# Start of a two-block transformer kernel: x loaded behind the second layer's first memory weights, squares of x on GpSimd, one key/value copy on VectorE

## The chip, the core and the metric

The kernel runs on one core of one Trainium2 chip. The metric is device time in microseconds (us) of one execution. Five engines each run their own instruction stream in order and meet only at semaphores: TensorE (PE, and PEld for its weight loads), VectorE (DVE), ScalarE (ACT), GpSimd (POOL) and SyncE (SP), which issues the DMAs here.

## The reference, cut to what matters

Two blocks of two layers each. The change touches only the first 80 us, where this is computed for the first block:

```python
for l in range(DEPTH):                       # DEPTH = 2, x is 512 x 1024, mem is 256 x 1024
    h = rms_norm(x, pre_norm[l])
    proj = h @ w_in[l]                       # all projections of the tokens
    ...
    mkv = rms_norm(mem, mem_norm[l]) @ w_mem_kv[l]   # keys and values of the memory
    mk, mv = jnp.split(mkv, 2, axis=-1)
```

`mkv` depends on no token, so the kernel computes it for both layers before anything else. `rms_norm` needs the sum of squares of each token, and that of `x` at the start is the one that the change moves to another engine.

## The kernel before

All matrices are kept transposed, with 1024 features as 8 chunks of 128 partitions. Products are made in split precision: each factor is a high part and a low part (the remainder), and a product is three matmuls (`mm3`, L353 to L355: high by high, low by high, high by low). For weights, ScalarE casts the high part (`wh`, L419) out of the loaded tile `wr`, and VectorE or GpSimd subtracts it to get the low part (`wl`, L421). For activations ScalarE writes `mh`, `xh` and VectorE `ml`, `xl`.

The program starts with these steps, in the order in which the code is written:

- `memory` (L903 on): for both layers l, two units u of 256 output columns, each from two halves of four chunks. A unit is 48 matmuls. Each half is one weight load of 512 KB (`wr`, one of two buffers). The row sums of squares of `mem` go through `square` (ScalarE squares, GpSimd adds), `ss_matmul` (L473, four matmuls against ones into `tp`) and `rsqrt` (nine tiny VectorE instructions, L364 to L372) to the factor `mr`. `finish` (L947 on) then copies the finished products out of PSUM with that factor (`mkv`, L952).
- `load_x`: four DMAs of 512 KB for x, called before the change in layer 0, behind the issue of the second unit's second weight half.
- `lead_load`: the weights of the first gate products, four loads (two halves of two units, called lead weights below: `wr_497`, `wr_507` for the first half of the features, `wr_517`, `wr_527` for the second). VectorE makes their low parts.
- `prenorm`: 16 chunks (8 feature chunks for each half of the tokens) through `pre_chunk`: ScalarE writes `xh`, VectorE `xl`, and `square` adds x squared to `sacc`.
- `lead` (192 matmuls into `sc`), then the token projections (`tok`, matmuls into `mm`), whose weight low parts (`wl_888` and on) GpSimd makes.

The written order isn't the final one: a scheduler of the framework reorders instructions on each engine by its own cost model when the program is built, so a change of engine or of call order can move others. Within an engine the final order is fixed, and an engine waits at the first instruction whose inputs aren't there. The weight tiles `wr` have two buffers, so a load of a token weight waits until GpSimd has split the one before the last; and all loads are issued from SP's single stream.

Of the kernel before, what the change touches and what calls it, by code (L numbers as in the profile page):

```python
# [23 lines left out]
F32 = mybir.dt.float32  # L24
F32R = mybir.dt.float32r
I32 = mybir.dt.int32
AF = mybir.ActivationFunctionType
OP = mybir.AluOpType
# [284 lines left out]
class Kern:  # L313
# [160 lines left out]
                                      start=i + tb == 0, stop=i == len(qs) - 1, skip_group_check=True)  # L474
        return p[:, 0, :2]

    def square(self, st, c, src, last=False):

        nc = self.nc
        if c == 0:  # L480
            st["acc"] = self.sq.tile([128, 256], F32, name="sacc", tag="sacc", bufs=4)
            nc.scalar.activation(st["acc"], src, AF.Square)
            return
        q = self.sq.tile([128, 512], F32, name="sq", tag="sq")[:, 0:256]
        nc.scalar.activation(q, src, AF.Square)
        if c < KC - 1 or not last:
            nc.gpsimd.tensor_tensor(st["acc"], st["acc"], q, op=OP.add)
        else:
            st["last"] = q
# [26 lines left out]
    def pre_chunk(self, st, c, g, sl):  # L516

        nc = self.nc
        hi, lo = [x[:, c, sl] for x in self.h]
        x = self.XT[:, c, sl]  # L520
        nc.scalar.activation(hi, x, AF.Copy, scale=self.gcol(g, c))
        nc.vector.scalar_tensor_tensor(lo, x, self.gcol(g, c), hi.bitcast(F32), op0=OP.mult, op1=OP.subtract)
        self.square(st, c, x)

    def rows(self, r, out=None):

# [376 lines left out]
    def memory(self):  # L903

        nc, ap = self.nc, self.ap
        self.mkv = []
        with self.tc.tile_pool(name="mem", bufs=1) as mp, self.tc.tile_pool(name="mem2", bufs=2) as mp2:
            mT = mp.tile([128, KC, N_MEM], F32, name="mT")
            load = lambda c: nc.sync.dma_start(mT[:, c:c + 2], ap["memT"][:, c:c + 2])
            load(0)  # L910
            r, late = None, []
            for l in range(self.nl1):
                kv = self.mempool.tile([128, MB, 512], F32, name=f"mkv{l}")
                self.mkv.append(kv)
                mh = mp2.tile([128, KC, N_MEM], F32R, name="mh", tag="mh")
                ml = mp2.tile([128, KC, N_MEM], F32R, name="ml", tag="ml")
                ps = []
                for u in range(2):
                    ps.append([(self.sc if (l + u) % 2 else self.mm)()[:, 0:256] for _ in range(MB)])
                    for half in range(2):  # L920
                        w = self.wload(ap["w_mem"][l, u, half], lo=nc.vector, raws=self.lead_pool if u else None,
                                       cut=l == 0 and u == 0)
                        if l == 0 and u == 0 and half == 0:
                            for c in (2, 4, 6):
                                load(c)
                        if l == 0 and u == 1 and half == 1:
                            self.load_x()
                        for i in range(4):
                            c = half * 4 + i
                            if u == 0:  # L930
                                g = self.gcol(G_MEM + l, c)
                                nc.scalar.activation(mh[:, c], mT[:, c], AF.Copy, scale=g)
                                nc.vector.scalar_tensor_tensor(ml[:, c], mT[:, c], g, mh[:, c].bitcast(F32),
                                                               op0=OP.mult, op1=OP.subtract)
                            for t in range(MB):
                                sl = slice(t * 128, (t + 1) * 128)
                                self.mm3(ps[u][t], (mh[:, c, sl], ml[:, c, sl]), w[i], c == 0, c == KC - 1)
                    if l == 0 and u == 0:
                        st = {}
                        for c in range(KC):  # L940
                            self.square(st, c, mT[:, c], last=True)
                    if late:
                        late.pop()()
                if l == 0:
                    r = self.sm(2, "mr")

                def finish(l=l, ps=ps, kv=kv):  # L947
                    if l == 0:
                        self.rms(st, r)
                    for u in range(2):  # L950
                        for t in range(MB):
                            nc.scalar.activation(kv[:, t, u * 256:(u + 1) * 256], ps[u][t], AF.Copy, scale=r[:, t:t + 1])  # L952
                late.append(finish)
            late.pop()()

# [657 lines left out]
```

## Time and profile before

| what | us |
|---|---|
| median of 3 runs | 2846.74 |
| range of the runs | 2845.9 to 2852.84 |
| the profiled execution's own time | 2845.98 |
| its span | 2844.0 |
| PE busy over the span | 2741.8 (96%) |

A timeline row reads: start, duration, engine, line, operation, output tile and input tiles, number of instructions merged, and in brackets how long the engine was idle before it and on whom it waited. A row for a stretch gives each engine's busy time in it, the clock that TensorE was granted (1.00 is 2.4 GHz, 0.50 is 1.2 GHz), the share of DMA capacity in use and GB/s. The profiled execution lies 0.8 us under the median, and 2.0 us of it lie outside the span.

### The profile page before, as it was taken

How to read it: one execution, taken by the hardware profiler on the slowest of the kernel's cores; microseconds unless marked ns; L12 is line 12 of the kernel's file. 1: busy time of each engine (PE TensorE's matmuls, PEld its weight loads, DVE VectorE, ACT ScalarE, POOL GpSimd, SP SyncE). 2: the span in 40 equal slices, each digit the busy share in tenths (PEclk: the TensorE clock that was granted, in tenths of full speed). 3: DMA queues.
4: the chain of work that ended last, by engine and by line, in shares of the span. 5: the costliest groups of instructions: out<-in, count | busy, mean ns of one | idle time of the engine just before them, and what ended most of it. 6: DMA issues, size and time to landing. Idle time of an engine off the chain costs nothing.

```text
span 2844.0 us, 42873 instructions
## 1 busy us (share of the span) xinstructions
PE 2741.8 (96%) x16080; PEld 2398.0 (84%) x16080; DVE 1412.6 (50%) x2988; ACT 1374.1 (48%) x2881; POOL 1356.5 (48%) x1327
## 2 busy tenths in 40 slices
PE   8999999999999999899999999999998899999998
PEld 8997899788888887898988888888887798888887
DVE  6589757986302266747630225312336747731132
ACT  5678547874333335657433334333334758433332
POOL 4553365424444455443544445444455543544545
PEclk9999999999999999999999999999999999999999
DMA  5111221112333222121223232233222120223332
GB/s 176 60 46 38 75 72 46 45 66 75 96 92 103 85 81 83 51 79 62 78 96 96 97 93 93 89 89 104 95 77 86 62 81 31 90 82 91 105 99 77
DMA packets 69280, 230.53 MB, mean 81 GB/s; under 512 B 8968, under 2 KB 11912, under 8 KB 68816
## 3 DMA queue, kind: packets, MB, share of 16 engines
q1 hardware_dynamic: 69072, 227.78, 24.5%
q8 instruction: 127, 2.08, 0.3%
q14 instruction: 81, 0.66, 0.1%
HBM read 225.51 MB, written 2.24 MB: 80 GB/s over the span
## 4 chain that ended last, share of the span: by engine, by line
PE 74%; DVE 15%; ACT 4%; issue 3%; POOL 2%; DMA 2%; SPq 0%; POOLq 0%; DVEq 0%; ACTq 0%
PE sc L354 11%; PE sc L353 11%; PE sc L355 11%; PE mm L355 11%; PE mm L353 11%; PE mm L354 11%; DVE xl L299 2%; PE sc L116 2%; PE tp L145 1%; DVE pl L149 1%; DVE XT L287 1%; DVE nm L192 1%; DVE E L204 1%; PE tp L817 1%; POOL wl L421 1%
## 5 line engine op out<-in xcount | busy, mean ns | idle before, releaser
L421 POOL TENSOR_TENSOR wl<-wr,wh 128x512 fp32r<-128x512 f32 x732 | 942.0, 1297 | 883.0 <-ACT wh L419 858.9
L419 ACT CAST wh<-wr 128x512 fp32r<-128x512 f32 x836 | 500.5, 612 | 722.8 <-PE sc L354 450.9
L354 PE MATMUL sc<-xl,wh 128*128 128x512 f32 (+1 forms) x1824 | 658.0, 361 | 16.3 <-DVE xl L299 16.2
L355 PE MATMUL sc<-xh,wl 128*128 128x512 f32 (+1 forms) x1824 | 654.5, 359 | 0.2 <-DVE wl L421 0.2
L353 PE MATMUL sc<-xh,wh 128*128 128x512 f32 (+1 forms) x1824 | 653.2, 360 | 0.0
L607 DVE TENSOR_TENSOR fg<-sc,R 128x512 f32<-128x512 f32 (+1 forms) x92 | 59.3, 644 | 747.6 <-PE sc L355 724.5
L354 PEld LDWEIGHTS sc<-xl,wh 128*128 128x128 f32 x1824 | 344.0, 189 | 72.1 <-DVE xl L299 20.7
L355 PEld LDWEIGHTS sc<-xh,wl 128*128 128x128 f32 x1824 | 344.2, 189 | 51.8 <-DVE wl L421 0.4
L353 PEld LDWEIGHTS sc<-xh,wh 128*128 128x128 f32 x1824 | 342.5, 189 | 51.5
L355 PE MATMUL mm<-ah,wl 128*128 128x512 f32 (+1 forms) x792 | 291.0, 367 | 6.5 <-POOL wl L421 6.5
L353 PE MATMUL mm<-ah,wh 128*128 128x512 f32 (+1 forms) x792 | 290.3, 367 | 1.9 <-ACT wh L419 1.9
L354 PE MATMUL mm<-al,wh 128*128 128x512 f32 (+1 forms) x792 | 289.3, 365 | 0.0
L353 PE MATMUL mm<-wh,xh 128*128 128x256 f32 x960 | 275.0, 286 | 0.0
L354 PE MATMUL mm<-wl,xh 128*128 128x256 f32 x960 | 273.2, 285 | 0.0
L355 PE MATMUL mm<-wh,xl 128*128 128x256 f32 x960 | 273.0, 284 | 0.0
L353 PE MATMUL mm<-xh,wh 128*128 128x512 f32 (+1 forms) x560 | 196.7, 353 | 10.5 <-DVE big L789 3.4
L355 PE MATMUL mm<-xh,wl 128*128 128x512 f32 (+1 forms) x560 | 194.8, 348 | 7.8 <-POOL wl L421 7.8
L354 PE MATMUL mm<-xl,wh 128*128 128x512 f32 (+1 forms) x560 | 193.9, 346 | 0.0
L354 PEld LDWEIGHTS mm<-wl,xh 128*128 128x128 f32 x960 | 184.1, 192 | 1.3
L353 PEld LDWEIGHTS mm<-wh,xh 128*128 128x128 f32 x960 | 183.9, 192 | 1.0
L355 PEld LDWEIGHTS mm<-wh,xl 128*128 128x128 f32 x960 | 184.0, 192 | 0.9
L355 PEld LDWEIGHTS mm<-ah,wl 128*128 128x128 f32 x792 | 149.2, 188 | 33.8 <-POOL wl L421 9.6
(348 smaller groups left out, 4878.1 us busy)
## 6 DMA issues: line engine op xcount, KB each, us to landing
wr<-in_ffn_in_dram SPq DMA_DIRECT2D x176, 512.0 KB, 3.3
wr<-in_ffn_out_dram SPq DMA_DIRECT2D x64, 512.0 KB, 3.6
wr<-in_mix_in_dram SPq DMA_DIRECT2D x56, 512.0 KB, 3.3
wr<-in_w_in_dram SPq DMA_DIRECT2D x48, 512.0 KB, 3.3
wr<-in_ffn_out_dram SPq DMA_DIRECT2D x32, 384.0 KB, 3.1
wr<-in_w_out_dram SPq DMA_DIRECT2D x16, 512.0 KB, 3.3
wr<-in_mix_out_dram SPq DMA_DIRECT2D x16, 512.0 KB, 3.3
Mb<-Md SPq DMA_DIRECT2D x16, 256.0 KB, 3.1
```

The lines of the kernel that those rows point to most:

```text
L116: nc.tensor.matmul(sc[:, e], q, kk[:, :n], start=j == 0, stop=j == len(self.K) - 1)
L145: nc.tensor.transpose(p[:, j * per + e], E[i + e][:, j * 128:(j + 1) * 128], self.k.ident)
L149: nc.vector.tensor_tensor(pl[:, :nk, sl], pv, ph[:, :nk, sl].bitcast(F32), op=OP.subtract)
L192: nc.vector.tensor_reduce(nm, sc, axis=AX.X, op=OP.max, negate=True)
L204: nc.vector.scalar_tensor_tensor(E[tb, 0], E[tb, 1], cc[:, i:i + 1], E[tb, 0], op0=OP.mult, op1=OP.add)
L299: self.put(self.nc.vector.scalar_tensor_tensor(lo, k.XT[:, j, sl], k.gcol(self.nxt[0], j), hi.bitcast(F32), op0=OP.mult, op1=OP.subtract))
L353: mm(out, lhs[0], rhs[0], start=start, stop=False, skip_group_check=shared)
L354: mm(out, lhs[0], rhs[1], start=False, stop=False, skip_group_check=shared)
L355: mm(out, lhs[1], rhs[0], start=False, stop=stop, skip_group_check=shared)
L419: nc.scalar.copy(hi[:, :m], raw[:, c:c + m])
L421: ins = eng.tensor_tensor(low[:, :m], raw[:, c:c + m], hi[:, :m].bitcast(F32), op=OP.subtract)
L607: nc.vector.tensor_tensor(g, ps[0], R[:, sl], op=OP.mult)
```

## The change

Three edits. `load_x` is called in the second layer's first unit, behind the issue of its second weight half, so that both halves of that unit are ahead of x on SP. `pre_chunk` squares x on GpSimd: one multiplication for each of the 16 chunks, and one addition for 14 of them, where ScalarE squared and GpSimd added. `finish` copies the second layer's four products out of PSUM on VectorE instead of ScalarE.

```diff
+    def square(self, st, c, src, last=False, pool=False):
         nc = self.nc
+        if pool:
+            if c == 0:
+                st["acc"] = self.sq.tile([128, 256], F32, name="sacc", tag="sacc", bufs=4)
+                nc.gpsimd.tensor_tensor(st["acc"], src, src, op=OP.mult)
+                return
+            q = self.sq.tile([128, 512], F32, name="sq", tag="sq")[:, 0:256]
+            nc.gpsimd.tensor_tensor(q, src, src, op=OP.mult)
+            nc.gpsimd.tensor_tensor(st["acc"], st["acc"], q, op=OP.add)
+            return
...
-        self.square(st, c, x)
+        self.square(st, c, x, pool=True)
...
-                        if l == 0 and u == 1 and half == 1:
+                        if (l, u, half) == (self.nl1 - 1, 0, 1):
                             self.load_x()
...
-                            nc.scalar.activation(kv[:, t, u * 256:(u + 1) * 256], ps[u][t], AF.Copy, scale=r[:, t:t + 1])
+                            o = kv[:, t, u * 256:(u + 1) * 256]
+                            if l:
+                                nc.vector.tensor_scalar(o, ps[u][t], r[:, t:t + 1], None, op0=OP.mult)
+                            else:
+                                nc.scalar.activation(o, ps[u][t], AF.Copy, scale=r[:, t:t + 1])
```

What the scheduler makes of it, at three places. Numbers in names tell buffers apart; brackets name whose semaphores an instruction waits for.

**Place 1, x.** SP at the loads of x. `wr_317` and `wr_359` are the second layer's first unit before, `wr_313` and `wr_355` the same two after. Before:

```order
L395 DMA wr_273<-in_w_mem_dram 128x1024 [waits DMAHW2_49]
L464 DMA XT_86<-in_xT_dram 128x1024 [waits DMAHW3_49]
L464 DMA XT_86<-in_xT_dram 128x1024 [waits DMAHW4_49]
L464 DMA XT_86<-in_xT_dram 128x1024 [waits DMAHW5_49]
L464 DMA XT_86<-in_xT_dram 128x1024 [waits DMAHW6_49]
L395 DMA wr_317<-in_w_mem_dram 128x1024 [waits DMAHW7_49,DVE_49]
L395 DMA wr_359<-in_w_mem_dram 128x1024 [waits DMAHW0_49,DVE_49]
```

SP at the same place after:

```order
L395 DMA wr_273<-in_w_mem_dram 128x1024 [waits DMAHW2_49]
L395 DMA wr_313<-in_w_mem_dram 128x1024 [waits DMAHW3_49,DVE_49]
L395 DMA wr_355<-in_w_mem_dram 128x1024 [waits DMAHW4_49,DMAHW7_49,DMAHW0_49,DVE_49]
L464 DMA XT_86<-in_xT_dram 128x1024 [waits DMAHW5_49]
L464 DMA XT_86<-in_xT_dram 128x1024 [waits DMAHW6_49]
L464 DMA XT_86<-in_xT_dram 128x1024 x2
L395 DMA wr_423<-in_w_mem_dram 128x1024 [waits DMAHW1_49,DVE_49]
```

The four loads of x now stand behind a weight load that waits for VectorE to free its buffer.

**Place 2, POOL and SP behind the squares.** `wl_888`, `wl_892`, `wl_898`, `wl_902` belong to the first token unit (`wr_885`, `wr_895`), `wl_1061` and `wl_1065` to the next (`wr_1058`). POOL before:

```order
L487 TENSOR_TENSOR sacc_580<-sacc_580,sq_609 128x256 [waits Activation_49,Pool_49]
L487 TENSOR_TENSOR sacc_580<-sacc_580,sq_614 128x256 [waits Activation_49,Pool_49]
L421 TENSOR_TENSOR wl_888<-wr_885,wh_887 128x512 [waits DMAHW3_49,PE_49,Activation_49]
L421 TENSOR_TENSOR wl_892<-wr_885,wh_891 128x512 [waits PE_49,Activation_49]
L421 TENSOR_TENSOR wl_898<-wr_895,wh_897 128x512 [waits DMAHW4_49,PE_49,Activation_49]
```

POOL after; 24 more multiplications and additions of the same two kinds stand ahead of these rows, 30 in all since the first load of x:

```order
L487 TENSOR_TENSOR sacc_580<-sacc_580,sq_599 128x256 [waits Pool_49]
L486 TENSOR_TENSOR sq_609<-XT_86 128x256
L487 TENSOR_TENSOR sacc_580<-sacc_580,sq_604 128x256 [waits Pool_49]
L486 TENSOR_TENSOR sq_614<-XT_86 128x256
L487 TENSOR_TENSOR sacc_580<-sacc_580,sq_609 128x256 [waits Pool_49]
L487 TENSOR_TENSOR sacc_580<-sacc_580,sq_614 128x256 [waits Pool_49]
L421 TENSOR_TENSOR wl_888<-wr_885,wh_887 128x512 [waits DMAHW3_49,Activation_49]
L421 TENSOR_TENSOR wl_892<-wr_885,wh_891 128x512 [waits Activation_49]
L421 TENSOR_TENSOR wl_898<-wr_895,wh_897 128x512 [waits DMAHW4_49,DVE_49,Activation_49]
L421 TENSOR_TENSOR wl_902<-wr_895,wh_901 128x512 [waits DVE_49,Activation_49]
L421 TENSOR_TENSOR wl_1061<-wr_1058,wh_1060 128x512 [waits DMAHW7_49,DVE_49,Activation_49]
L421 TENSOR_TENSOR wl_1065<-wr_1058,wh_1064 128x512 [waits DVE_49,Activation_49]
```

SP at the lead weights before:

```order
L395 DMA wr_507<-in_w_in_dram 128x1024 [waits DMAHW6_49,DMAHW2_49,DVE_49]
L395 DMA wr_517<-in_w_in_dram 128x1024 [waits DMAHW5_49,DVE_49]
L395 DMA wr_527<-in_w_in_dram 128x1024 [waits DMAHW6_49,DVE_49]
L395 DMA wr_1058<-in_w_in_dram 128x1024 [waits DMAHW3_49,Pool_49]
L395 DMA wr_1068<-in_w_in_dram 128x1024 [waits DMAHW4_49,Pool_49]
L395 DMA wr_1192<-in_w_in_dram 128x1024 [waits DMAHW1_49,Pool_49]
```

SP at the lead weights after:

```order
L395 DMA wr_507<-in_w_in_dram 128x1024 [waits DMAHW6_49,DMAHW2_49,DVE_49]
L395 DMA wr_1058<-in_w_in_dram 128x1024 [waits DMAHW7_49,DMAHW3_49,Pool_49]
L395 DMA wr_1068<-in_w_in_dram 128x1024 [waits DMAHW4_49,DMAHW0_49,Pool_49]
L395 DMA wr_1192<-in_w_in_dram 128x1024 [waits DMAHW7_49,Pool_49]
L395 DMA wr_517<-in_w_in_dram 128x1024 [waits DMAHW5_49,DVE_49]
L395 DMA wr_527<-in_w_in_dram 128x1024 [waits DMAHW6_49,DVE_49]
```

The second half of the lead weights has moved behind three loads that wait for POOL, `wr_1192` for `wl_1065`.

**Place 3, DVE ahead of the second layer's second unit.** `wl_426` to `wl_464` are that unit's four low parts, the small rows between them the memory's `rsqrt`. Before:

```order
L372 SCALAR_TENSOR_TENSOR mr_311<-rnt_407,mr_311 128x2 [waits DVE_49]
L421 TENSOR_TENSOR wl_320<-wr_317,wh_319 128x512 [waits DMAHW7_49,Activation_49]
L421 TENSOR_TENSOR wl_324<-wr_317,wh_323 128x512 [waits Activation_49]
L421 TENSOR_TENSOR wl_362<-wr_359,wh_361 128x512 [waits DMAHW0_49,Activation_49]
L421 TENSOR_TENSOR wl_366<-wr_359,wh_365 128x512 [waits Activation_49]
L421 TENSOR_TENSOR wl_426<-wr_423,wh_425 128x512 [waits DMAHW1_49,Activation_49]
```

DVE after, where eleven `xl` stand ahead of `wl_426` (these rows begin at the eighth of them, and the other four splits of the layer stand earlier):

```order
L531 SCALAR_TENSOR_TENSOR xl_85<-XT_86,gains_87,xh_84 128x256 [waits DMAHW0_49,Activation_49]
L531 SCALAR_TENSOR_TENSOR xl_85<-XT_86,gains_87,xh_84 128x256 [waits Activation_49]
L531 SCALAR_TENSOR_TENSOR xl_85<-XT_86,gains_87,xh_84 128x256
L531 SCALAR_TENSOR_TENSOR xl_85<-XT_86,gains_87,xh_84 128x256 [waits Activation_49]
L364 TENSOR_SCALAR rnx_406<-tp_401 128x2 [waits PE_49]
L421 TENSOR_TENSOR wl_426<-wr_423,wh_425 128x512 [waits DMAHW1_49,Activation_49]
L365 TENSOR_SCALAR mr_307<-rnx_406 128x2 [waits DVE_49]
```

The splits of the first unit moved ahead of x's work, those of the second unit behind most of it, and `mr` behind both. On PE the lead's rows are reordered too, so that only 53 of its 192 matmuls stand ahead of the first one that reads the second half of the lead weights (`wh_519`), with two token matmuls (on `wh_887` and `wl_888`) among them, and the other 139 behind it; from its 442nd instruction on PE's order is that of before.

## Rows read from the trace of the kernel before

**Rows 1.** The page's busy time of each engine, share of the span, instructions.

```profile
PE 2741.8 (96%) x16080; PEld 2398.0 (84%) x16080; DVE 1412.6 (50%) x2988; ACT 1374.1 (48%) x2881; POOL 1356.5 (48%) x1327
```

**Rows 2.** Stretches: PE, PEld, DVE, ACT, POOL busy; PEclk; DMA share; GB/s.

```profile
16.70:22.40 5.70, 5.70 (x50) 5.67 (x49) 5.70 (x14) 5.70 (x16) 0.65 (x1) 1.00 0.97 385
22.90:28.00 5.10, 0.50 (x2) 0.30 (x2) 4.90 (x15) 3.30 (x8) 2.40 (x4) 0.82 0.02 6
28.00:32.90 4.90, 4.88 (x23) 4.88 (x24) 3.67 (x6) 3.40 (x8) 0.00 (x0) 0.50 0.66 182
32.90:41.50 8.60, 8.60 (x73) 8.60 (x73) 5.91 (x9) 7.52 (x19) 3.41 (x4) 1.00 0.46 151
41.50:65.90 24.40, 24.18 (x201) 23.84 (x200) 10.30 (x21) 9.91 (x23) 13.94 (x16) 1.00 0.36 119
65.90:90.00 24.10, 24.10 (x204) 24.10 (x203) 10.11 (x37) 10.01 (x17) 15.17 (x29) 1.00 0.13 45
```

**Rows 3.** The chain that ended last, in order of time: start, duration, what.

```profile
27.27 0.70 DVE wl L421
28.02 0.58 PE sc L354
```

**Rows 4.** PE's timeline at the lead's last matmuls and the first token matmul.

```profile
65.65 0.28 PE L354 MATMUL sc<-xl,wh 128*128 128x256 f32 x1
65.77 0.28 PE L355 MATMUL sc<-xh,wl 128*128 128x256 f32 x1
65.89 0.28 PE L353 MATMUL mm<-wh,xh 128*128 128x256 f32 x1
```

**Rows 5.** SP's timeline: the first load of x and the fourth memory unit's load.

```profile
6.60 0.33 SPq L464 DMA_DIRECT2D XT<-in_xT_dram  x1
13.13 0.33 SPq L395 DMA_DIRECT2D wr<-in_w_mem_dram  x1
```

**Rows 6.** Loads in 0 to 100 us, median to landing; then all `wr` loads, extremes.

```profile
wr<-in_w_in_dram SPq DMA_DIRECT2D x13, 512.0 KB, 3.4
DMA to landing us min/median/max: 3.3/5.2/8.3
```

**Rows 7.** POOL's instructions by line: duration ns min/median/max, starts, shape.

```profile
L487 POOL TENSOR_TENSOR sacc<-sacc,sq x116: 727/742/1302, 7.8 to 2827.8; 128x256 f32<-128x256 f32 x116
L1112 POOL TENSOR_TENSOR dsq<-pa x6: 1042/1042/1044, 161.3 to 569.6; 128x512 f32<-128x512 f32 x6
L421 POOL TENSOR_TENSOR wl<-wr,wh x6: 1289/1295/1307, 51.2 to 59.1; 128x512 fp32r<-128x512 f32 x6
```

**Rows 8.** POOL's timeline while DVE works too.

```profile
41.51 1.28 POOL L487 TENSOR_TENSOR sacc<-sacc,sq 128x256 f32<-128x256 f32 x1 [0.80 <-ACT sq L485]
42.94 0.74 POOL L487 TENSOR_TENSOR sacc<-sacc,sq 128x256 f32<-128x256 f32 x1
43.76 0.80 POOL L487 TENSOR_TENSOR sacc<-sacc,sq 128x256 f32<-128x256 f32 x1
```

**Rows 9.** DVE's timeline in the same stretch.

```profile
42.11 0.96 DVE L522 SCALAR_TENSOR_TENSOR xl<-XT,gains,xh 128x256 fp32r<-128x256 f32 x1
43.23 0.73 DVE L522 SCALAR_TENSOR_TENSOR xl<-XT,gains,xh 128x256 fp32r<-128x256 f32 x1 [0.16 <-ACT xh L521]
44.05 1.07 DVE L421 TENSOR_TENSOR wl<-wr,wh 128x512 fp32r<-128x512 f32 x1
```

**Rows 10.** DVE's timeline with POOL idle.

```profile
17.83 0.68 DVE L421 TENSOR_TENSOR wl<-wr,wh 128x512 fp32r<-128x512 f32 x1
18.43 3.25 DVE L933 SCALAR_TENSOR_TENSOR ml<-mT,gains,mh 128x256 fp32r<-128x256 f32 x8
27.27 2.50 DVE L421 TENSOR_TENSOR wl<-wr,wh 128x512 fp32r<-128x512 f32 x4
```

**Rows 11.** ACT's timeline: two copies of keys and values, four weight casts.

```profile
29.02 0.83 ACT L952 ACTIVATE mkv<-sc,mr 128x256 f32<-128x256 f32 x2
49.91 2.17 ACT L419 CAST wh<-wr 128x512 fp32r<-128x512 f32 x4
```

**Rows 12.** DVE's scaled copies out of PSUM later on: duration ns min/median/max.

```profile
L1061 DVE TENSOR_SCALAR unit<-mm,r x8: 473/480/484, 95.5 to 414.3; 128x256 f32<-128x256 f32 x8
```

More of the change, by code (lines that the diff above doesn't have):

```diff
@@ L475, in ss_matmul @@
         return p[:, 0, :2]
-    def square(self, st, c, src, last=False):
+    def square(self, st, c, src, last=False, pool=False):
         nc = self.nc
+        if pool:
[7 more added lines that the diff above has]
+            return
         if c == 0:
```

## The prediction

> **What bounds the kernel now.** The page's first part comes first: PE is busy for 96% of the span and the other engines for about half [rows 1], so time is to be gained or lost only where PE waits or runs slowly. The table by stretch shows where that is at the beginning [rows 2]. PE works through layer 0's memory products until 22.4 us, then has 0.50 us of work in 5.1 us, then runs 23 matmuls in 4.9 us at a granted clock of 0.50 (1.2 GHz), and is full at 2.4 GHz from 32.9 us on. The chain in order of time names the cause: the first matmul at 28.02 followed a VectorE weight split that ended there [rows 3]; VectorE and ScalarE had been at x until then. The idle 5.1 us are one loss, the slow clock behind them another: 23 matmuls took 0.213 us each instead of 0.12 [rows 2, 4], which is 2.1 us. So the change aims at 5.1 + 2.1 = 7.2 us. The reader is to see that PE is full afterwards, and that the lead ends at 65.89 [rows 4]: everything that follows is PE bound and in the same order, so the change's effect is the shift of that point.
>
> **x comes later.** x was issued at 6.60 [rows 5]. Now its loads stand behind `wr_355`, which waits for VectorE's splits of the load whose buffer it takes. The same wait let `wr_359` go at 13.13 before [rows 5], and nothing ahead of it changes. A 512 KB load takes 3.3 us at the least [rows 6], and the one in front of x occupies the DMA engines for 0.52 MB / 385 GB/s = 1.36 us [rows 2]. So the first of x lands at about 13.13 + 3.3 + 1.36 = 17.8 us, an estimate good to perhaps 1.3 us. That alone costs nothing: PE is at layer 0 until 22 us, and layer 1's first unit is now split ahead of x's work.
>
> **The squares on GpSimd.** They are 16 multiplications and 14 additions of 128x256. The addition costs 0.74 us alone [rows 7]. A multiplication of one tile with itself stands in the trace at 128x512 alone: 1.04 us, where two tiles take 1.29 [rows 7]. From 0.74 to 1.29 another 256 columns cost 0.55, which leaves 0.19 fixed; for one tile that gives 0.19 + (1.04 - 0.19)/2 = 0.62 us. The bounds are 0.52 (half of 1.04) and 0.74 (as two tiles). I take 0.62. Starts lie 0.08 us further apart than durations (42.94 to 43.76 for 0.74) [rows 8]. Alone the 30 would take 16 x 0.70 + 14 x 0.82 = 22.7 us, from 17.8 to 40.5. ScalarE loses 16 squares, but it isn't what is waited for.
> The Trainium skill's page "GPSIMD Engine Reference", section 3.1, gives a two-input operation some 2.6 cycles per element, because both inputs come through one port. If a square counts as two inputs it costs 0.74, and the sum rises by 16 x 0.12 = 1.9 us. The 1.04 us row speaks against that.
>
> **VectorE and GpSimd take turns.** This is the main term. At 41.51 GpSimd's addition needed 1.28 instead of 0.74, and the `xl` that VectorE began at 42.11 ended at 43.07, which is 0.28 behind the addition's end at 42.79. The next addition ended at 43.68 and the next `xl` at 43.96, again 0.28 later; the one after at 44.56 and the weight split at 45.12, 0.56 later [rows 8, 9]. With GpSimd idle eight such instructions take 3.25 us and four splits 2.50, so 0.41 and 0.63 each [rows 10]. So while both have work, one VectorE instruction passes per GpSimd instruction. GpSimd is held up by only 0.14 behind an `xl` (42.79 to 42.94 is 0.15), and for a split I take 0.56 - 0.14 = 0.42. A turn is GpSimd's mean (16 x 0.62 + 14 x 0.74)/30 = 0.68 plus that: 0.82 us with an `xl` or `ml`, 1.10 with a split.
> Ahead of `wl_426` VectorE has 24 such instructions from 17.83 on: 5 splits, 8 `ml`, 11 `xl`. In turns they take 19 x 0.82 + 5 x 1.10 = 21.1 us from GpSimd's first result at 18.4, so to 39.5 us; alone they would take 10.9. PE's first unit of layer 1 rides on the `ml` and hides in it. Its second unit begins at about 40.1 us.
> From there to the end of `mr`, GpSimd has 5 squares or additions left and then `wl_888` and `wl_892` at 1.29 [rows 7]: 5 x 0.68 + 2 x 1.29 + 4 splits x 0.42 + 4 `xl` x 0.14 = 8.2, so `mr` is done at 47.7.
> By the Trainium skill's page "SBUF — State Buffer", section "SBUF: two separate sides", a VectorE instruction with two SBUF inputs and a GpSimd one exclude each other for the whole instruction. The exclusion is what the rows show; by the whole instruction the turns would be longer, which is the third rival below.
>
> **What follows from that.** ScalarE stands before `mr` with layer 0's four copies queued, and behind them the lead's casts: 4 x 0.41 = 1.7, three casts x 0.54 = 1.6 [rows 11], so PE begins the lead at about 51.0 us instead of 41.5. ScalarE's next three casts (to `wh_901`) last until 52.7, and GpSimd can start `wl_898` at 52.1. Its four splits take 4 x 1.29 [rows 7] plus two turns with VectorE's splits, 0.84, to 58.1. Only then SP may issue `wr_1192`, and half a microsecond later `wr_517`. It lands 3.4 us on [rows 6], at 62.0; its cast (0.54) ends at 62.6. PE has 53 lead matmuls for the time from 51 on, some 9 us at the slow clock's start, and then waits.
> From 62.6 PE has the other 139 lead matmuls: x 0.12 [rows 4] = 16.7, to 79.3. The wait of some 3 us ahead of them may drop the clock as the one of 5.1 us did: 0 to 2.1 us. I take 2.1, since 3 is nearer to that row than to no wait, and get 81.4. Three token matmuls (0.36) are already done then. The shift is 81.4 - 65.9 - 0.4 = 15.1 us.
>
> **The copies on VectorE.** Four of 0.48 us [rows 12] replace 1.7 us on ScalarE. On VectorE they stand ahead of the lead's splits, between 48 and 51 us; PE waits for ScalarE's casts then, which come no earlier. Nothing is added; without that cover it would be 1.9 us. Nothing later changes: the tables and token evacuations keep their distance to the lead's end.
>
> **The sum.** 2845.98 + 15.1 = 2861.1 for the profiled execution; the median lies 0.8 above it, 2861.9. I predict 2862 us. Squares at 0.52 or 0.74 move it by -1.6 or +1.9, the landing of x by 1.3 either way, the clock by -2.1: 2857 to 2865.
>
> **The rivals.**
> First, no turns: GpSimd and VectorE run beside each other and only the queues count. The 30 end at 40.5, `wl_892` at 43.1, `wr_1058` lands 3.4 later at 46.5, its casts and splits end at 47.0 + 2 x 1.29 = 49.6, `wr_517` is issued at 50.1, lands at 53.5, and is cast at 54.0. With 16.7 and the clock's 2.1 the lead ends at 72.8, a shift of 6.5: 2853 us. Rows 8 and 9 speak against it; for it speaks that they show one stretch of three turns.
> Second, faster: the change does what its place suggests, PE goes from layer 0 straight through layer 1 into the lead, and -7.2 us give 2839.5. For that `wh_519` must be there when PE needs it. A lead that ends no later than before has it at 65.9 + 0.4 - 16.7 = 49.6; the chain from the last square to it takes 54.0 - 40.5 = 13.5, so the 30 would have to end at 36.1, at 0.61 us from start to start. That is the point from which it decides. Even squares at 0.52 give 0.71. It needs x some microseconds earlier as well.
> Third, whole instructions exclude each other: turns of 0.68 + 0.41 = 1.09 and 0.68 + 0.63 = 1.31. The 24 turns take 19 x 0.27 + 5 x 0.21 = 6.2 us more, the 8 after them 2.0, GpSimd's splits 0.4: 8.6 more, 2870.5 us. For it speaks the addition at 41.51, held up by 0.54 of a split's 0.63; against it the 0.15 us gap at 42.79.
>
> **How the numbers follow.** Chances: the forecast 0.64, no turns 0.18, faster 0.04, whole instructions 0.14. A difference under 0.3% (8.5 us) is about what a measurement of this kernel can't tell from no change: 2838.2 to 2855.3 is the same. The first rival lies in it with its clock term either way (2851 to 2853), the second with its full gain too, so most of it; that makes 0.20 the same, 0.02 faster, 0.78 slower. The range takes in the first rival's lower end with some allowance for an earlier x, and the third: 2850 to 2871.
>
> **What would show it.** Right: GpSimd's squares and additions run unbroken from about 18 to 44 us with VectorE's `xl` at 0.7 to 0.9 us instead of 0.41; PE idle ahead of the second unit of layer 1 until about 40 and ahead of the lead until about 51; `wr_517` issued behind 58 us, and PE waiting for `wh_519`; the first token matmul after the last of the lead at about 81 instead of 65.9, and the same distance from there to the end. Wrong: `xl` at 0.41 us beside a busy GpSimd (first rival), or lead weights that land ahead of 46 us (second).

## The result

| | before | after |
|---|---|---|
| median, four runs each, side by side | 2848.49 us | 2863.64 us |
| range | 2845.9 to 2852.84 | 2860.93 to 2866.79 |
| profiled execution, its span | 2845.98, 2844.0 | 2862.66, 2860.9 |

The ratio is 1.0052, with a 95% interval of 1.0040 to 1.0064: slower by about 15 us, 1.6 us above the forecast of 2862.

**The profile after.** TensorE's busy time is unchanged (answers to [rows 1]), so the 15 us are waiting:

```profile
PE 2742.3 (96%) x16080; PEld 2398.9 (84%) x16080; DVE 1423.8 (50%) x2992; ACT 1368.0 (48%) x2861; POOL 1369.8 (48%) x1343
```

By stretches (columns as in [rows 2]):

```profile
16.30:22.10 5.80, 5.80 (x49) 5.80 (x49) 5.80 (x8) 5.80 (x14) 4.40 (x5) 1.00 1.01 390
22.10:30.00 7.90, 6.68 (x52) 6.17 (x50) 7.90 (x10) 7.90 (x20) 7.74 (x11) 1.00 0.57 206
30.00:40.00 10.00, 0.61 (x4) 0.52 (x4) 10.00 (x15) 1.38 (x3) 9.84 (x13) 0.71 0.00 0
40.00:46.00 6.00, 0.00 (x0) 0.00 (x0) 6.00 (x9) 0.00 (x0) 5.92 (x7) 0.50 0.47 162
46.00:52.00 6.00, 3.73 (x20) 3.73 (x21) 4.06 (x17) 4.16 (x9) 0.78 (x2) 0.56 0.31 100
82.00:106.00 24.00, 24.00 (x202) 24.00 (x202) 8.15 (x28) 11.63 (x20) 13.95 (x19) 1.00 0.14 46
```

The hole that the change aimed at is nearly filled: from 22.1 to 30 TensorE works for 6.68 of 7.9 us, where it had 0.50 of 5.1 before. But a larger hole stands behind it. From 30 to 46 us TensorE and ScalarE do almost nothing while VectorE is never idle and GpSimd hardly, and TensorE comes out of it near the half clock (0.56 from 46 to 52).

TensorE's timeline names what it waited for: the last matmul row of the memory's mean square, the first one of layer 1's second unit, the first one of the lead, a wait in the lead, and the lead's last.

```profile
29.41 0.50 PE L473 MATMUL tp<-ones,sq 128*128 128x1 f32 x4
48.27 0.58 PE L353 MATMUL mm<-wh,mh 128*128 128x256 f32 x1 [15.87 <-ACT mkv L965]
55.42 0.28 PE L353 MATMUL sc<-xh,wh 128*128 128x256 f32 x1
59.12 0.39 PE L355 MATMUL sc<-xh,wl 128*128 128x256 f32 x1 [0.84 <-DVE wl L421]
80.06 0.28 PE L355 MATMUL sc<-xh,wl 128*128 128x256 f32 x1
```

ScalarE, on which it waited, waited itself for the mean square `mr`:

```profile
47.74 0.84 ACT L965 ACTIVATE mkv<-mm,mr 128x256 f32<-128x256 f32 x2 [16.36 <-DVE mr L372]
62.61 1.14 ACT L419 CAST wh<-wr 128x512 fp32r<-128x512 f32 x2 [5.45 <-DMA wr<-in_w_in_dram]
```

And VectorE, which makes `mr`, was at the low parts of x beside GpSimd's squares. First VectorE, then GpSimd, and last the end of `mr` and the lead's first matmul in the kernel before:

```profile
28.70 8.91 DVE L531 SCALAR_TENSOR_TENSOR xl<-XT,gains,xh 128x256 fp32r<-128x256 f32 x11
37.54 0.15 DVE L364 TENSOR_SCALAR rnx<-tp 128x2 f32<-128x2 f32 x1
37.61 1.03 DVE L421 TENSOR_TENSOR wl<-wr,wh 128x512 fp32r<-128x512 f32 x1
39.76 0.56 DVE L366 TENSOR_TENSOR rnt<-mr 128x2 f32<-128x2 f32 x1
47.56 0.15 DVE L372 SCALAR_TENSOR_TENSOR mr<-rnt,mr 128x2 f32<-128x2 f32 x1
```

```profile
17.70 0.81 POOL L483 TENSOR_TENSOR sacc<-XT 128x256 f32<-128x256 f32 x1 [2.02 <-DMA XT<-in_xT_dram]
28.46 1.54 POOL L486 TENSOR_TENSOR sq<-XT 128x256 f32<-128x256 f32 x2
29.97 1.77 POOL L487 TENSOR_TENSOR sacc<-sacc,sq 128x256 f32<-128x256 f32 x2
44.10 2.66 POOL L421 TENSOR_TENSOR wl<-wr,wh 128x512 fp32r<-128x512 f32 x2
56.37 1.55 POOL L421 TENSOR_TENSOR wl<-wr,wh 128x512 fp32r<-128x512 f32 x1 [0.16 <-ACT wh L419]
```

```profile
27.06 0.15 DVE L372 SCALAR_TENSOR_TENSOR mr<-rnt,mr 128x2 f32<-128x2 f32 x1
41.54 0.28 PE L353 MATMUL sc<-xh,wh 128*128 128x256 f32 x1
```

Eleven `xl` take 8.91 us, 0.81 each, where eight like ones took 3.25 with GpSimd idle, 0.41 each [rows 10]. GpSimd's 30 instructions run unbroken from 17.70 to 44.1. So the chain is: beside GpSimd's squares VectorE gets one `xl` done per square or addition, and between 37.6 and 44.2 us ten instructions, `mr`'s tiny steps among them, beside six; `mr` is done at 47.71, where it was at 27.2 before; ScalarE empties layer 0's PSUM tiles behind it; TensorE's next unit needs these tiles. The lead begins at 55.42 instead of 41.54, 13.9 us later, and ends at 80.06 instead of 65.77, 14.3 later: nearly all of the loss lies ahead of it.

### The profile page after: what moved, and what is told of

It reads as the page before. It is cut to its first block, busy times and chain, and to the rows that moved or that the text cites. A ratio compares the mean times of both kernels' runs of the same rounds, so it can differ in the third digit from the quotient of the medians.

```text
span 2860.9 us, 42871 instructions
## 1 busy us (share of the span) xinstructions
PE 2742.3 (96%) x16080; PEld 2398.9 (84%) x16080; DVE 1423.8 (50%) x2992; ACT 1368.0 (48%) x2861; POOL 1369.8 (48%) x1343
## 4 chain that ended last, share of the span: by engine, by line
PE 73%; DVE 16%; ACT 4%; issue 3%; POOL 2%; DMA 1%; SPq 0%; POOLq 0%; DVEq 0%; ACTq 0%
PE sc L354 11%; PE sc L353 11%; PE sc L355 11%; PE mm L355 11%; PE mm L353 11%; PE mm L354 11%; DVE xl L299 2%; PE sc L116 2%; PE tp L145 1%; DVE pl L149 1%; DVE XT L287 1%; DVE nm L192 1%; DVE E L204 1%; PE tp L826 1%; POOL wl L421 1%
```

## The experiments

All ratios are to the kernel before, run beside them on the same chip. The kernels were run in groups, not all on one chip, so two rows are compared by their ratios; "the lead" is the time of its first and last matmul in the profile.

| kernel | median us | ratio (95%) | the lead |
|---|---|---|---|
| before, after | 2848.5, 2863.6 | 1, 1.0052 (1.0040 to 1.0064) | 41.5 to 65.8, 55.4 to 80.1 |
| e2_sq_only | 2860.75 | 1.0039 (1.0026 to 1.0052) | 49.9 to 76.4 |
| e3_x_only | 2850.49 | 1.0009 (1.0000 to 1.0018) | 44.7 to 67.9 |
| e4_cp_only | 2856.60 | 1.0030 (1.0019 to 1.0040) | 41.1 to 73.0 |
| e1_sq_act | 2855.88 | 1.0027 (1.0017 to 1.0037) | 44.2 to 71.5 |
| e9_no_cp | 2863.07 | 1.0054 (1.0039 to 1.0069) | 57.6 to 80.7 |
| e7_order | 2863.38 | 1.0054 (1.0039 to 1.0069) | 56.2 to 83.4 |
| e5_psum | 2861.94 | 1.0046 (1.0029 to 1.0062) | 53.2 to 78.7 |
| e8_order_psum | 2859.64 | 1.0042 (1.0027 to 1.0057) | 53.8 to 78.6 |
| e10_rms_early | 2860.57 | 1.0045 (1.0033 to 1.0058) | 50.3 to 79.3 |
| v4_x_rms | 2846.62 | 0.9997 (0.9988 to 1.0006) | 38.7 to 64.2 |
| v3_x_psum_rms | 2847.35 | 0.9999 (0.9990 to 1.0008) | 38.8 to 63.6 |
| e12_best_sq | 2858.04 | 1.0036 (1.0023 to 1.0050) | 50.8 to 75.5 |

The first theory was that the squares on GpSimd make the whole loss, by VectorE's turns and the late `mr`. The rivals: x's later load or the copies carry part of it; or it is the place of the lead's weights behind GpSimd's work in SP's queue.

### One part alone, or one part undone

e1_sq_act, the change without the squares:

```diff
-        self.square(st, c, x, pool=True)
+        self.square(st, c, x)
```

> The changed kernel with the 16 squares back on ScalarE; x still comes later and VectorE still copies the second layer's keys and values. If the squares on GpSimd are the whole loss (VectorE in turns with GpSimd, so the memory's mean square late, so layer 0's copies late, so TensorE idle to 48.3 us), all 15 us come back and something of the earlier memory weights shows: 2840 to 2849 us, and TensorE begins the second layer's second unit before 36 us. If x's later load or the copies on VectorE carry the loss, it stays at 2855 or above.

e2_sq_only, the squares alone: the line with `pool=True` in the kernel before.

> The kernel before with the 16 squares on GpSimd and nothing else; x stands ahead of the second layer's weights as before, ScalarE makes all copies, and in SyncE's order the lead's last two weights stand ahead of the three token weights. If VectorE's turns with GpSimd make the loss by way of the mean square and layer 0's copies: 2859 to 2867 us, TensorE again idle for over 10 us until just behind those copies. If the place of the lead's weights behind GpSimd's work in SyncE's queue makes it: 2852 or less here, where they are not behind it.

e3_x_only, x's place alone:

```diff
-                        if l == 0 and u == 1 and half == 1:
+                        if (l, u, half) == (self.nl1 - 1, 0, 1):
```

> The kernel before with x loaded behind the second layer's first memory weights and nothing else. If the squares make the whole loss: 2842 to 2849 us, a gain of at most the 2 to 5 us that the second layer's first weights come earlier, if TensorE's end of the head follows from it. If the later x carries a part of the loss, 2851 or above: xh and xl later, the lead later.

e4_cp_only, the copies alone:

```diff
-   nc.scalar.activation(kv[:, t, u * 256:(u + 1) * 256], ps[u][t], AF.Copy, scale=r[:, t:t + 1])
+   o = kv[:, t, u * 256:(u + 1) * 256]
+   if l:
+       nc.vector.tensor_scalar(o, ps[u][t], r[:, t:t + 1], None, op0=OP.mult)
+   else:
+       nc.scalar.activation(o, ps[u][t], AF.Copy, scale=r[:, t:t + 1])
```

> The kernel before with the second layer's four copies on VectorE and nothing else. If the copies are off the path (ScalarE only frees 4 x 0.5 us behind the last product): within 2845 to 2850 us, no difference that can be told. If they carry a part of the loss (VectorE held behind them for the products' end, with the lead's splits in its queue): 2851 or above.

The squares alone cost 12.7 us, as the theory had it and without the lead's weights behind GpSimd's work. But it met its range by another path than the one that it named: TensorE's holes were not ahead of layer 1's second unit but at the first sum of x and at a split of layer 1's first unit, which stand behind x in that order:

```profile
30.93 0.37 PE L473 MATMUL tp<-ones,sacc 128*128 128x1 f32 x1 [7.83 <-POOL sacc L487]
36.60 0.58 PE L354 MATMUL sc<-wl,mh 128*128 128x256 f32 x1 [4.02 <-DVE wl L421]
```

x's place alone cost 2.4 us, between the two ranges that were expected of it. The theory that the squares are everything fell: with them undone 7.8 us remained, not 0, and the copies alone cost 8.5. The parts' losses, 12.7 + 2.4 + 8.5 = 23.6, are more than the change's 15.1. So the parts hide one another.

What the second layer's four copies, 0.44 us each, can do, on VectorE and then GpSimd and TensorE in e4_cp_only:

```profile
40.98 0.88 DVE L963 TENSOR_SCALAR mkv<-mm,mr 128x256 f32<-128x256 f32 x2 [1.59 <-PE mm L355]
41.77 4.10 DVE L421 TENSOR_TENSOR wl<-wr,wh 128x512 fp32r<-128x512 f32 x4
45.80 5.78 DVE L531 SCALAR_TENSOR_TENSOR xl<-XT,gains,xh 128x256 fp32r<-128x256 f32 x4
```

```profile
45.29 6.01 POOL L421 TENSOR_TENSOR wl<-wr,wh 128x512 fp32r<-128x512 f32 x4
```

```profile
53.69 0.58 PE L355 MATMUL sc<-xh,wl 128*128 128x256 f32 x1 [4.32 <-DVE wl L421]
```

The last two copies stand in VectorE's queue ahead of work that is ready, and wait 1.59 us for TensorE's unit. Meanwhile ScalarE, rid of them and in a new order that has GpSimd's casts ahead of those for the lead's second half, has made GpSimd's casts early enough for its splits to begin at 45.29 instead of 51.2 [rows 7], while VectorE still has four `xl`. These now go in turns with splits of 1.3 us: 1.44 each. The lead's own low part comes behind them, TensorE waits 4.32 us, and then runs at a granted clock of 0.53 (54 to 60 us). The rows fit the same mechanism as with the squares, with other work on GpSimd. The cast of that low part's weights was done at 48.04, and VectorE stood at the `xl` until 51.58 and at tiny steps of a mean square behind them. No further run tested this reading.

### Which link carries it in the changed kernel

e5_psum puts the two halves of a unit into one PSUM tile, so that layer 1's second unit needs no tile of layer 0:

```diff
-   ps.append([(self.sc if (l + u) % 2 else self.mm)()[:, 0:256] for _ in range(MB)])
+   pt = (self.sc if (l + u) % 2 else self.mm)()
+   ps.append([pt[:, t * 256:(t + 1) * 256] for t in range(MB)])
...
-   self.mm3(ps[u][t], (mh[:, c, sl], ml[:, c, sl]), w[i], c == 0, c == KC - 1)
+   self.mm3(ps[u][t], (mh[:, c, sl], ml[:, c, sl]), w[i], c == 0 and t == 0, c == KC - 1, shared=True)
```

> The changed kernel with the two column halves of a unit of the memory products in one PSUM tile instead of two, so that the second layer's second unit no longer needs the two tiles that ScalarE empties only behind the mean square. If TensorE's 15.9 us of idle time ahead of that unit are a link of the loss: TensorE begins it at about 39 us instead of 48.3, the lead at about 50 instead of 55, and the lead's last two weights (two places earlier in SyncE's order here) let it end 3 to 6 us earlier: 2857 to 2861 us. If the end of the lead hangs on the chain from GpSimd's squares to the lead's weights or on the mean square alone: 2862 to 2866 us, the idle time only moves behind the unit.

e7_order issues the token weights behind the lead's on SP, as before the change:

```diff
+   with self.tc.issue_after(self.lead_dma) if self.lead_n in (1, 2, 3) else nullcontext():
        ins = nc.sync.dma_start(raw[:, c:e], src[:, c:e])
...
```

> The changed kernel with SyncE's order of the kernel before for the weight loads: the lead's last two loads ahead of the three token weights, nothing else. If the lead's weights behind GpSimd's splits were what set the lead's end (the sum's fifth step), they come 10 us earlier and the lead ends some 7 us earlier: 2854 to 2858 us. If the late start of the lead (TensorE idle to 48.3 us for layer 0's copies) sets it, the weights are there in time either way: 2861 to 2866 us.

e8_order_psum has both edits.

> Both edits together: one PSUM tile per unit of the memory products, and the lead's last two weights ahead of all token weights in SyncE's order. If the two are chains in parallel, each covering the other: 2852 to 2857 us here where each alone gives less. If the mean square, late by GpSimd and VectorE in turns, holds ScalarE's casts for the lead anyway: the lead begins at about 50 us and ends 5 us earlier than in the changed kernel, 2857 to 2861 us.

e9_no_cp gives the copies back to ScalarE:

```diff
-                            if l:
+                            if False:
                                 nc.vector.tensor_scalar(o, ps[u][t], r[:, t:t + 1], None, op0=OP.mult)
```

> The changed kernel with the second layer's four copies on ScalarE again (SyncE's order then has the lead's last two weights one token weight earlier). In the kernel before the copies on VectorE alone cost 8.5 us, and the squares there alone 12.7, x's place 2.4: 23.6 together, where the whole change costs 15.1. If the copies are covered behind the squares (the prediction's step), this stays within 2 us of the changed kernel: 2861 to 2866 us. If they cost their own 8.5 us here too: 2853 to 2857 us.

Taking back the copies (e9) or SP's order (e7) gains nothing that can be told in the changed kernel; the intervals leave room for some 5 us, less than the copies' own 8.5. SP's issue of `wr_517` with the change, and in e7_order:

```profile
58.49 0.33 SPq L395 DMA_DIRECT2D wr<-in_w_in_dram  x1
```

```profile
58.17 0.33 SPq L398 DMA_DIRECT2D wr<-in_w_in_dram  x1
```

Ahead of the token weights it goes hardly earlier, because its tile is freed by VectorE's splits of the lead's first weights, and these began at 56.05 and 56.86, behind the late copies. In the changed kernel it goes 0.03 us behind the second of them, which beside a split of GpSimd's took 1.78 us instead of 0.68:

```profile
56.69 1.78 DVE L421 TENSOR_TENSOR wl<-wr,wh 128x512 fp32r<-128x512 f32 x1
```

e7 has a cost of its own: the lead's last load, issued at 59.37 with token weights close behind it, landed only at 65.3, and TensorE waited for its cast:

```profile
65.99 0.58 PE L353 MATMUL sc<-xh,wh 128*128 128x256 f32 x1 [2.02 <-ACT wh L426]
```

With the second unit's PSUM link cut (e5), TensorE ran all of that unit but its first matmul from 40.29, 8 us earlier, but began the lead only 2.2 earlier. TensorE, then VectorE and GpSimd in e5_psum:

```profile
40.29 0.58 PE L354 MATMUL mm<-wl,mh 128*128 128x256 f32 x1 [6.71 <-DVE wl L421]
52.01 0.58 PE L353 MATMUL mm<-wh,xh 128*128 128x256 f32 x1 [4.55 <-ACT mkv L966]
```

```profile
46.69 1.23 DVE L370 TENSOR_TENSOR rnt<-rnt,rnx 128x2 f32<-128x2 f32 x1
49.33 1.21 DVE L371 SCALAR_TENSOR_TENSOR rnt<-rnt 128x2 f32<-128x2 f32 x1
50.94 0.14 DVE L372 SCALAR_TENSOR_TENSOR mr<-rnt,mr 128x2 f32<-128x2 f32 x1
```

```profile
45.20 5.33 POOL L421 TENSOR_TENSOR wl<-wr,wh 128x512 fp32r<-128x512 f32 x4
```

The gain was given back on VectorE: the earlier unit let ScalarE cast weights for GpSimd earlier, so `mr`'s last steps took turns with splits of 1.3 us instead of squares of 0.8, and `mr` came at 51.1 instead of 47.7. And the link itself moved rather than went: the second row of TensorE is a token matmul that stands ahead of the lead and waits 4.55 us for the same copies behind `mr`. e5 lies within the uncertainty of the changed kernel; e8 may be a few microseconds faster, which its interval doesn't settle, but it isn't the 2852 to 2857 us of two chains that hide each other.

### The mean square early, and the squares in the best head

e10_rms_early writes the memory's mean square behind layer 0's products instead of behind layer 1's first unit:

```diff
                 if l == 0:
                     r = self.sm(2, "mr")
+                    self.rms(st, r)

                 def finish(l=l, ps=ps, kv=kv):
-                    if l == 0:
-                        self.rms(st, r)
```

> The changed kernel with one line moved: the memory's mean square is written behind layer 0's products instead of behind the second layer's first unit, so that its matmul stands ahead of that unit on TensorE (as it did in the kernel before) and its nine small steps stand among VectorE's ml and first xl instead of behind eleven xl. If the late mean square is the link by which the squares on GpSimd cost time: it is done at about 30 us instead of 47.7, ScalarE's copies and the lead's casts come that much earlier, TensorE begins the second unit at about 39 to 41 us and the lead ends 6 to 9 us earlier: 2854 to 2858 us. If VectorE's turns with GpSimd hold the xl and the lead's splits just the same (then GpSimd's weight splits, let go earlier, run against the last xl): 2859 to 2864 us.

v4_x_rms is e3_x_only with the same line moved.

> The kernel before with x loaded later and with the memory's mean square written behind layer 0's products; squares and copies stay on ScalarE. With x later alone TensorE waited 4.3 us for x's own first sum, which stood ahead of the second layer's second unit on it, and 2.9 us for layer 0's copies behind the late mean square. If these two are what took back the gain of x's later load: 2841 to 2846 us, a gain of 2 to 7 us on the kernel before. If the head is bound by the split and cast work itself: 2847 to 2851 us, no difference.

v3_x_psum_rms is that with the PSUM edit of e5_psum.

> As the kernel with x later and the mean square early, and the memory products' two halves of a unit in one PSUM tile besides. If the copies still hold the second unit in that kernel, this is faster by the part that they hold it: 2840 to 2845 us. If the early mean square alone has already freed them: equal to it within 1.5 us.

e12_best_sq is v3_x_psum_rms with `pool=True`, nothing else.

> The kernel with x later, the mean square early and one PSUM tile per unit (2847.4 us), with the 16 squares on GpSimd added to it and nothing else: what the squares cost when the late mean square, the two PSUM tiles, the copies on VectorE and (but for one place) the order of the loads are all out of the way. If those links were the cost, within 4 us of it: 2847 to 2851 us. If it is VectorE in turns with GpSimd as such (27 splits, ml and xl at about 0.8 us instead of 0.41 to 0.63 ahead of the lead's own splits, so that these begin at about 50 us): 2855 to 2861 us, most of the whole change's 15 us.

e10 missed: TensorE did begin the second unit at 40.1, as expected of the link, but the time is that of the rival. `mr` came at 37.9 us, not at 30, because each of its steps took a turn too, and the lead's splits then stood behind the last seven `xl`, four of them in turns with GpSimd's splits, 1.4 us each. v4 and v3 agree within 1 us, so the PSUM tiles no longer hold there; both lie some 3 us under e3, with intervals that overlap, and are no different from the kernel before; no version here beats it. e12 against v3 is the cleanest measurement: two programs whose source differs only in who squares. Squares on GpSimd cost 2858.04 - 2847.35 = 10.7 us there, within the range expected of turns, and 10.5 by the ratios; from their intervals I estimate 6 to 15. One thing else differs in what the scheduler made of it: one token weight is loaded ahead of the lead's last weights. TensorE's holes, first in v3_x_psum_rms and then in e12_best_sq:

```profile
30.87 0.38 PE L353 MATMUL mm<-wh,mh 128*128 128x256 f32 x1 [2.42 <-ACT wh L419]
31.60 0.38 PE L354 MATMUL mm<-wl,mh 128*128 128x256 f32 x1 [0.34 <-DVE wl L421]
```

```profile
40.10 0.58 PE L353 MATMUL mm<-wh,mh 128*128 128x256 f32 x1 [6.57 <-ACT wh L419]
43.31 0.58 PE L354 MATMUL mm<-wl,mh 128*128 128x256 f32 x1 [2.63 <-DVE wl L421]
```

and why ScalarE's casts were late, the copies ahead of them in the one and the other:

```profile
28.74 0.84 ACT L965 ACTIVATE mkv<-mm,mr 128x256 f32<-128x256 f32 x2 [2.87 <-DVE mr L372]
```

```profile
37.97 0.84 ACT L965 ACTIVATE mkv<-mm,mr 128x256 f32<-128x256 f32 x2 [11.30 <-DVE mr L372]
```

`mr` is 9.2 us later (37.97 against 28.74), the second unit's first matmul 9.2, and the wait for VectorE's split adds to it: the lead begins 12.0 us later (50.81 against 38.81) and ends 11.9 later. From 26 to 42 us an `xl` takes 958 ns on average in e12 and 666 in v3.

## Why the prediction came out right, and where it did not

**x comes later:** forecast to land at 17.8; GpSimd began at 17.70 after waiting for it. "That alone costs nothing" was nearly so: 2.4 us alone, with an interval that begins at no loss. What cost there was came with the order: in e3 x's first sum stood ahead of the second unit on TensorE (4.3 us) and the mean square behind the first unit (2.9 us for the copies). v4, without these two waits, is faster than e3, but not clear of its interval.

**The squares:** right, though the changed kernel alone seems to say otherwise. There their median is 0.79 us and none took less than 0.789, against 0.62 forecast for a square alone. But each of them stood beside an `xl`, `ml` or split. In e12 some follow one of the mean square's tiny steps; GpSimd, then VectorE:

```profile
33.70 0.61 POOL L486 TENSOR_TENSOR sq<-XT 128x256 f32<-128x256 f32 x1
34.27 0.79 POOL L486 TENSOR_TENSOR sq<-XT 128x256 f32<-128x256 f32 x1
35.02 0.72 POOL L487 TENSOR_TENSOR sacc<-sacc,sq 128x256 f32<-128x256 f32 x1
```

```profile
33.08 0.68 DVE L369 TENSOR_TENSOR rnt<-mr 128x2 f32<-128x2 f32 x1
33.68 0.91 DVE L531 SCALAR_TENSOR_TENSOR xl<-XT,gains,xh 128x256 fp32r<-128x256 f32 x1
34.51 0.56 DVE L370 TENSOR_TENSOR rnt<-rnt,rnx 128x2 f32<-128x2 f32 x1
```

The `xl` begun at 33.68 waits through the first square and so stands ahead of the second. Behind a tiny step a square takes 0.61 and an addition 0.72; behind an `xl` a square takes 0.79. So the term of 0.62 holds, and an `xl` holds a square up by 0.18 us, a little more than the forecast's 0.14; in the changed kernel two squares beside `xl` begin 0.75 us apart, against 0.62 + 0.14. The case that the prediction worked out beside the Trainium skill's page "GPSIMD Engine Reference", section 3.1, and set aside, a square as dear as an addition of two tiles, isn't borne out. The 30 ended at 44.1 (forecast 44).

**VectorE in turns:** right in size and in place, 0.81 per `xl` against 0.82; `wl_426` done at 38.6 (39.5), `mr` at 47.71 (47.7). A split's turn was 1.15 us, from 23.14 to 24.29, against 1.10. e12 against v3 shows that the squares on GpSimd cost the time, and that it is lost ahead of the lead, not in GpSimd's queue behind it; that the turns are how, the rows show, each `xl` and each step of `mr` by itself. The third rival, whole instructions excluding each other in both directions, falls: an `xl` took 0.81, not its 1.09.

**"Its second unit begins at about 40.1 us":** the step that failed. It was costed by VectorE's split alone; the trace has 48.27. The unit's two PSUM tiles still held layer 0's products, which ScalarE empties behind `mr`. The prediction had these copies in its next sentence, queued before the lead's casts, and counted them as a delay of the casts, not as the release of a tile that TensorE needs. So the lead began at 55.42, not 51.0. In e5, where that unit has a tile of its own, all but its first matmul ran from 40.29: the split was sized rightly, and the other release was left out.

**The wait for the lead's last weights, and the clock behind it:** they fell away. The cast of `wr_517` began at 62.61, where it was forecast to end at 62.6, but TensorE, later itself, didn't stand for it: its only hole in the lead is the 0.84 us at 59.12, for a split. The low clock came ahead of the lead and not in it: from 46 to 52 us it was 0.56, behind the wait of 15.87 us, and from 55.42 on 1.00. And it was VectorE's split that released that load, not GpSimd's work ahead of it on SP: the load went 0.03 us behind the split. (Two token matmuls, not three, stood within the lead, which is 0.1 us.) So the lead began 4.4 us later than forecast and took 24.8 us (55.42 to 80.18) instead of 30.4 (51.0 to 81.4): two terms wrong in opposite directions, and a sum that came out within 2 us. That it came so close is luck.

**The copies on VectorE:** "nothing is added" holds in the changed kernel as far as can be told (e9: 2863.07 against 2863.64). "Without that cover it would be 1.9 us" was wrong by a factor of more than four (e4: 8.5): the copies' own time was counted, not who waits behind a waiting copy and what ScalarE, relieved and reordered, lets go on GpSimd.

**The faster rival:** a head with x later, ScalarE squaring and the mean square early does fill the 5.1 us hole (v4: 6.54 us of TensorE's work from 22 to 30 instead of 3.35) and yet gains at most some microseconds: the lead begins 2.9 us earlier and ends 1.5 earlier. Behind the filled hole stand a wait of 2.4 us for a cast and a lower clock after it (0.83 from 30 to 40 us), and a wait of 1.1 in the lead. TensorE's longest waits there are for ScalarE's casts; no run tried to make them faster.

**Left open:** the profiled spans differ by 16.9 us, where the lead's end differs by 14.3. The rest comes behind the lead and is no more than single executions of the kernel before differ by (2845.9 to 2852.84). And there was no way here to take the turns away while GpSimd keeps the squares, so the 10.7 us are measured against squares on ScalarE, not against squares on GpSimd without turns.

## What to carry to other kernels

Before work goes to GpSimd because GpSimd is idle, count VectorE's instructions in that stretch: with both reading SBUF, VectorE got one to two instructions done per GpSimd instruction, and a short one waited like a long one. Work that looked free cost 11 to 13 us (e12 against v3, and e2). For each unit of matmuls list all that releases it, its PSUM tiles included, and take the latest. An instruction that waits in an in-order queue costs what stands behind it, and an engine that is relieved starts other work earlier, so price a move by both.

## What was not expected of the hardware

A short instruction of VectorE waits as long as a long one. The steps of the mean square on 128x2 elements take 0.15 to 0.17 us with GpSimd idle; beside squares and additions they took 0.56 to 0.71, and beside splits of 1.3 us 1.1 to 1.2. The first step, `rnx`, which reads PSUM instead of SBUF, took 0.15 at 37.54 while GpSimd was busy. What the size of VectorE's instruction does set is how long GpSimd's next one takes: a square 0.61 us behind a tiny step and 0.79 behind an `xl` (e12), and 1.06 to 1.13 behind a split (the changed kernel). The Trainium skill's page "SBUF — State Buffer", section "SBUF: two separate sides", says that whichever of the two starts first keeps the shared ports for its whole instruction, if VectorE's has two SBUF inputs or runs in a two-port mode. For the waits of VectorE's steps the rows agree, while GpSimd lost only 0.18 us at a square to an `xl` that takes 0.41 alone.
